# Emitting the assembly of the chunk inverses behind the products of the mixer's h and behind the first scores of retention

## The chip, the core and the metric

The kernel runs on one core of one Trainium2 chip. The metric is the device time of one execution in microseconds (us). A core has five engines, each with its own instruction stream, executed in order: TensorE (PE, with its weight loads shown as PEld), VectorE (DVE), ScalarE (ACT), GpSimd (POOL) and SyncE (SP), which here only issues DMAs. An instruction waits for semaphores of other engines or of DMAs, and everything behind it in the same stream waits with it.

## The reference

All values are float32; 512 tokens, width 1024. Two layers of a first kind of block (the second kind, which follows twice, isn't touched):

```python
for l in range(DEPTH):                       # DEPTH = 2
    ...                                      # a first feed-forward
    h = modulate(rms_norm(x), sh2, sc2)
    z = h @ w_in[l]
    z_a, z_b, z_c = split_cols(z, [RWKV_COLS, MLA_COLS, RET_COLS])
    o_a = rwkv7_mixer(z_a, ...)
    o_b = mla_mixer(z_b, ...)
    o_c = retention_mixer(z_c, ...)
    mixed = jnp.concatenate([o_a, o_b, o_c], axis=-1) @ w_out[l]
    x = x + g2[:, None, :] * mixed
    ...                                      # a second feed-forward
```

The rwkv mixer is a recurrence over tokens, with a state of 64x64 for each head and direction. Retention, per head and direction, is `scores = einsum(q, k) * dmat` and `einsum(scores, v)` over chunks; MLA is softmax attention over low-rank keys and values, with a rotary key `kpe` of 32 columns.

## The kernel before

A float32 product is written as three products of rounded halves (hi·hi, hi·lo, lo·hi). A weight lands by DMA in a buffer `raw`; ACT casts it to its high half, DVE or POOL subtracts that for the low half (both halves are tiles named `wr`), and PE multiplies. Weights come through a list, `self.wplan`, in a fixed order: `in_b` (five pieces), `in_kpe`, `w_uq_pe`, `w_ukv_v` (512 KB), `w_kq` (four pieces of 320 KB), then the output weights. Their DMAs are issued by SP, in stream with all other DMAs of SP.

The first mixer (`mixer1`, phase "mix1") runs two Python generators against each other in `merge`: the main one is `rwkv`, the other (`fill`) is everything else. Each `yield n` of the main one says how much other work is wanted at that place, and `merge` then draws on `fill`, whose own yields say how much they gave. The order in which calls are made, together with the allocator of tiles, sets the order of the engines' streams.

`fill` makes in turn: `rwkv_z` (the rwkv products with h), `ret_z` (the retention products), `mla_z` (the five `in_b` pieces and kpe, again products with h), `retention` (two head pairs j, with `mla_norms` between them), and `mla`. `retention` begins by making the stacks `kq` for its scores: casts on ACT and subtractions on DVE that write tiles named `mix_r_x`. Then, for each of four chunks c, it makes four score products on PE, two multiplications by the decay mask on DVE, and two value products one chunk later, and yields `RET_FILL` (2.5).

The main generator, `rwkv`, prepares the rwkv operands (`rwkv_prep`), calls `rwkv_inverse` and then runs the heads (`rwkv_heads`). `rwkv_inverse` inverts 64x64 triangular matrices, one for each chunk, head and direction: it takes 32x32 diagonal blocks through DRAM (`rw_d`) into another layout, inverts them on DVE by back substitution in `zb` (`mix_big_w`), and writes them back to DRAM. Two DMAs (`xa`) and sixteen DMAs of 32 KB (`xt`) on SP then bring the inverted blocks back. Behind these stands `yield INV_WAIT` (20), and then `rwkv_blocks` for j = 0 and 1, which assembles the off-diagonal blocks: for each j and direction 16 products of 32x32 (y), two copies on ACT, 16 products of 32x32 (z), two copies on ACT. That is 128 such products of 32x32 in all (the trace records each as two), and the heads begin after them. In the stream of PE before, the 20 units drawn at `INV_WAIT` end after `in_b[2]`; `in_b[3]`, `in_b[4]` and kpe, 24 matmuls each, are interleaved with the blocks and with the first work of the heads.

Of the kernel before, what the change touches and what calls it, by code (L numbers as in the profile page):

```python
# [37 lines left out]
RET_FILL = 2.5  # L38
# [197 lines left out]
class Build:  # L236
# [606 lines left out]
    def rwkv_inverse(self, os_):  # L843


        nc = self.nc
        dr, dz, dzt = (self.dram_p.tile([P, 1024], F32, tag=self.nm("rw_d"), name=self.nm("rw_d")) for _ in range(3))
        u = {}
        for j, o in enumerate(os_):
            for d in range(2):  # L850
                us = self.slot()
                u4 = us.rearrange("p (c h t) -> p c h t", c=4, h=2)
                pus = [self.aux_ps()[:, :256].rearrange("p (c t) -> p c t", c=4) for hh in range(2)]
                for par in range(2):
                    for c in range(4):
                        for hh in range(2):
                            rows = slice(hh * 64, hh * 64 + 64)
                            q = o["qm"][rows, d, c, par, par, :]
                            p = o["pr"][rows, d, c, 0, par * 64:par * 64 + 64]
                            a, b = (q, p) if d == 0 else (p, q)  # L860
                            nc.tensor.matmul(pus[hh][par * 64:par * 64 + 64, c, :], a, b, start=True, stop=True)
                for hh in range(2):
                    up = self.mask("tri")[:, :64].unsqueeze(1).to_broadcast([P, 4, 64])
                    nc.vector.scalar_tensor_tensor(u4[:, :, hh, :], pus[hh], -1.0, up, ALU.mult, ALU.mult)
                u[j, d] = us
                u3 = us.rearrange("p (m t) -> p m t", t=64)
                ud = self.slot()
                ud3 = ud[:, :256].rearrange("p (m t) -> p m t", t=32)
                for r0 in range(0, P, 32):
                    h0 = r0 % 64  # L870
                    nc.scalar.copy(ud3[r0:r0 + 32], u3[r0:r0 + 32, :, h0:h0 + 32])
                to = dr.rearrange("(j m d q) (r c) -> j d q r m c", j=2, m=8, d=2, r=32)[j, d]
                self.nc.sync.dma_start(to.rearrange("q r m c -> (q r) m c"), ud[:, :256].rearrange("p (m c) -> p m c", m=8))
                yield 2

        zb, zt = self.big_t(), self.big_t()
        self.nc.sync.dma_start(zb, dr)
        yield 6
        z3 = zb.rearrange("p (r c) -> p r c", r=32)
        for c in range(30, 0, -1):  # L880
            n = 31 - c
            tmp = self.small_t(256, "inv_t")
            t3 = tmp[:, :c * n].rearrange("p (r c) -> p r c", r=c)
            nc.vector.tensor_mul(t3, z3[:, 0:c, c:c + 1].to_broadcast([P, c, n]),
                                 z3[:, c:c + 1, c + 1:].to_broadcast([P, c, n]))
            nc.vector.tensor_add(z3[:, 0:c, c + 1:], z3[:, 0:c, c + 1:], t3)
            if c % 5 == 0:
                yield INV_STEP
        nc.vector.memset(zb[:, ::33], 1.0)
        self.nc.sync.dma_start(dz, zb)  # L890
        nc.vector.tensor_copy(zt.rearrange("p (c r) -> p c r", c=32), z3.rearrange("p r c -> p c r"))
        self.nc.sync.dma_start(dzt, zt)
        rows = lambda z, d: z.rearrange("(jm d q) (r c) -> d q r jm c", jm=16, d=2, r=32)[d]
        xa = []
        for d, z in enumerate((dzt, dz)):
            t = self.slot()
            self.nc.sync.dma_start(t.rearrange("p (m t) -> p m t", m=16), rows(z, d).rearrange("q r jm c -> (q r) jm c"))
            xa.append(t.rearrange("p (j m t) -> p j m t", j=2, m=8))
        xt = [[self.slot() for d in range(2)] for j in range(2)]
        for j in range(2):  # L900
            for d, z in enumerate((dz, dzt)):
                x3 = xt[j][d].rearrange("p (m t) -> p m t", t=64)
                for q in range(4):
                    r0, h0 = q * 32, q % 2 * 32
                    self.nc.sync.dma_start(x3[r0:r0 + 32, :, h0:h0 + 32], rows(z, d)[q, :, j * 8:j * 8 + 8, :])
                    if q % 2 != d:
                        nc.gpsimd.memset(x3[r0:r0 + 32, :, 32 - h0:64 - h0], 0.0)
        yield INV_WAIT
        for j in range(2):
            yield from self.rwkv_blocks(xt[j], [t[:, j] for t in xa], [u[j, d] for d in range(2)])  # L910
        return xt
# [450 lines left out]
    def retention(self, l, z, out, between):  # L1362
        nc = self.nc
        lg = self.small_t(16, "ret_lg")
        nc.scalar.activation(lg[:, 8:16], self.rows[:, 4 + 8 * l:12 + 8 * l], AF.Exp)
        nc.vector.tensor_scalar(lg[:, 0:8], lg[:, 8:16], -1.0, None, ALU.mult)
        lag = self.big_t()[:, :896]
        nc.sync.dma_start(lag, self.d["lag"])
        pn = self.aux_ps()
        kq = []  # L1370
        for j in range(2):
            dm = [self.ret_decay(lag, lg, j * 2 + hh) for hh in range(2)]
            py, pts = self.aux_ps(), None
            for c in range(5):
                if j == 0 and c in (0, 2):
                    kq.append((self.stack_q(z["k"][c // 2]), self.stack_k(z["q"][c // 2])))
                last = pts
                if c < 4:
                    scs, pts = [self.aux_ps() for hh in range(2)], []
                    for hh in range(2):  # L1380
                        self.stacked(scs[hh], *kq[j], hh, slice(c * P, (c + 1) * P), ALL)
                    for hh in range(2):
                        pt = self.slot()
                        nc.vector.scalar_tensor_tensor(pt, scs[hh], 0.125, dm[hh][:, 384 - c * P:896 - c * P],
                                                       ALU.mult, ALU.mult)
                        pts.append(pt)
                if c > 0:
                    for hh in range(2):
                        v = ((c - 1) % 2) * 256 + (j * 2 + hh) * 64
                        nc.tensor.matmul(py[hh * 64:hh * 64 + 64], z["v"][(c - 1) // 2][:, v:v + 64], last[hh],  # L1390
                                         start=c == 1, stop=c == 4)
                yield RET_FILL
            sq, o = self.slot(), z["g"][j]
            nc.scalar.activation(sq, py, AF.Square)
            nc.vector.scalar_tensor_tensor(o, py, self.v(f"gn_g{l}", j), o, ALU.mult, ALU.mult)
            yield 2.5
            self.head_sums(sq, pn, j * 8)
            yield 1
            if j == 0:
                yield from between  # L1400
        vv = self.small_t(64, "rs_v")
        nc.vector.tensor_scalar(vv[:, :16], pn[:, :16], 1.0 / 64, 1e-5, ALU.mult, ALU.add)
        rn = self.rsqrt(vv[:, :16], 16)
        yield 2
        for j in range(2):
            pb = self.head_bcast(rn[:, j * 8:j * 8 + 8], 2, 0)
            out[j] = z["g"][j]
            nc.vector.tensor_mul(out[j], out[j], pb)
            yield 1
# [16 lines left out]
    def mixer1(self, l):  # L1426
# [11 lines left out]
        def fill():  # L1438
            yield from self.rwkv_z(l, h, ps, dv, za)
            zc = yield from self.ret_z(l, h)  # L1440
            zb = yield from self.mla_z(l, h)
            yield from self.retention(l, zc, oc, self.mla_norms(l, zb))
            self.stage(2)
            yield from self.mla(l, zb, ob, (oa, oc))

        with self.phase("mix1"):
            self.stage(0)
            h, ps = self.modulated(1, [self.wget() for i in range(2)])
            self.lend_x()
            dv = self.derived(l)  # L1450
            self.merge(self.rwkv(l, za, dv, oa), fill())
            self.split_all((oa, oc))

            def update(j, po, sl):
                nc.vector.scalar_tensor_tensor(self.x[j][:, sl], po[:, sl], self.mod[:, 40 + j:41 + j],
                                               self.x[j][:, sl], ALU.mult, ALU.add)

            self.out_proj(lambda j: self.wget(), oa + oc + ob, update, "halves")
# [527 lines left out]
```

## Time and profile before

| | us |
|---|---|
| three runs | 3542.39, 3544.21, 3565.40 |
| their median | 3544.21 |
| the profiled execution, whole time | 3542.78 |
| its span | 3541.0 |
| PE busy in it | 3416.4 (96% of the span) |
| ACT busy, DVE busy | 1437.5, 2095.7 |
| mean granted TensorE clock | 0.982 |

The span is what the profiler sees between the first and last instruction; 1.8 us lie around it. Within the span, the first mixer's part of interest is at 526 to 606 us for layer 0 and at 1695 to 1767 us for layer 1. All operations are recorded by one helper, so every row has the same line (L138), and tiles are told by their names: `mix_h_x` is the h of the mixer, `mix_s`, `mix_s_x`, `mix_s_y` and `x` are scratch tiles, `mix_r_x` rounded operands, `mix_big_w` the wide tiles of the back substitution and of retention's decay masks, `ps` PSUM.

### The profile page before, as it was taken

How to read it: one execution, taken by the hardware profiler on the slowest of the kernel's cores; microseconds unless marked ns; L12 is line 12 of the kernel's file. 1: busy time of each engine (PE TensorE's matmuls, PEld its weight loads, DVE VectorE, ACT ScalarE, POOL GpSimd, SP SyncE). 2: the span in 40 equal slices, each digit the busy share in tenths (PEclk: the TensorE clock that was granted, in tenths of full speed). 3: DMA queues.
4: the chain of work that ended last, by engine and by line, in shares of the span. 5: the costliest groups of instructions: out<-in, count | busy, mean ns of one | idle time of the engine just before them, and what ended most of it. 6: DMA issues, size and time to landing. Idle time of an engine off the chain costs nothing. (4 is left out here: it accounts for less than half of the span.)

```text
span 3541.0 us, 45671 instructions
## 1 busy us (share of the span) xinstructions
PE 3416.4 (96%) x17394; PEld 2786.5 (79%) x17394; DVE 2095.7 (59%) x4153; ACT 1437.5 (41%) x2644; POOL 279.2 (8%) x344
## 2 busy tenths in 40 slices
PE   6999998999999999999899999999999999999998
PEld 5888876788888888887678888887788887778887
DVE  7954785757964544467576544466754446774445
ACT  3233554454233423245345423245443344444333
POOL 2000152100000000015310000000100000000000
PEclk9999998999999999999899999999999999999999
DMA  7933322015852222232201222221122222212222
GB/s 271 330 136 107 126 78 63 24 44 200 328 185 99 87 96 97 99 119 83 75 13 48 78 97 96 99 86 68 54 95 95 96 100 72 70 60 101 96 97 76
DMA packets 132876, 375.73 MB, mean 106 GB/s; under 512 B 37712, under 2 KB 41072, under 8 KB 132656
## 3 DMA queue, kind: packets, MB, share of 16 engines
q1 hardware_dynamic: 127808, 359.48, 29.5%
q0 software_dynamic: 3776, 12.32, 1.0%
q8 instruction: 136, 2.23, 0.2%
q10 hardware_dynamic: 1072, 1.01, 0.1%
q14 instruction: 84, 0.69, 0.1%
HBM read 362.27 MB, written 10.49 MB: 105 GB/s over the span
## 5 line engine op out<-in xcount | busy, mean ns | idle before, releaser
L138 ACT CAST wr<-raw 128x512 fp32r<-128x512 f32 (+2 forms) x1054 | 642.4, 611 | 1484.7 <-PE ps L138 1377.4
L138 DVE TENSOR_TENSOR wr<-raw,wr 128x512 fp32r<-128x512 f32 (+1 forms) x1004 | 681.0, 680 | 741.4 <-ACT wr L138 719.7
L138 PE MATMUL ps<-ff_h,wr 128*128 128x512 f32 (+1 forms) x4296 | 961.1, 385 | 9.9 <-ACT ff_h L138 7.4
L138 PEld LDWEIGHTS ps<-ff_h,wr 128*128 128x128 f32 x4296 | 794.8, 190 | 172.2 <-ACT ff_h L138 9.9
L138 PE MATMUL ps<-mlp_r,wr 128*128 128x512 f32 (+1 forms) x3120 | 699.3, 386 | 2.1 <-ACT mlp_r L138 2.1
L138 PEld LDWEIGHTS ps<-mlp_r,wr 128*128 128x128 f32 x3120 | 578.5, 188 | 121.2 <-ACT mlp_r L138 3.0
L138 PE MATMUL ps<-ff_r,wr 128*128 128x512 f32 (+1 forms) x2238 | 483.0, 377 | 0.0
L138 PEld LDWEIGHTS ps<-ff_r,wr 128*128 128x128 f32 x2238 | 403.6, 188 | 77.6
L138 PE MATMUL ps<-mix_r,wr 128*128 128x512 f32 (+1 forms) x1104 | 274.9, 399 | 2.4 <-DVE mix_s L138 1.8
L138 PE MATMUL ps<-mix_h_x,wr 128*128 128x512 f32 (+2 forms) x1104 | 261.1, 396 | 3.5 <-ACT mix_h_x L138 2.2
L138 PEld LDWEIGHTS ps<-mix_h_x,wr 128*128 128x128 f32 (+1 forms) x1104 | 202.5, 200 | 53.8 <-issue 4.5
L138 PEld LDWEIGHTS ps<-mix_r,wr 128*128 128x128 f32 (+1 forms) x1104 | 198.6, 185 | 56.1 <-issue 4.8
L138 DVE SCALAR_TENSOR_TENSOR ff_big<-ff_big,ff_big 128x1024 f32<-128x1024 f32 x144 | 176.6, 1238 | 15.2 <-DMA ff_big<-in_w_ada 14.5
L138 DVE SCALAR_TENSOR_TENSOR ff_s<-ff_s,ps 128x512 f32<-128x512 f32 x176 | 120.1, 683 | 82.2 <-PE ps L138 78.1
L138 DVE SCALAR_TENSOR_TENSOR x<-ps,hg,x 128x512 f32<-128x512 f32 (+1 forms) x102 | 73.3, 719 | 78.6 <-PE ps L138 78.4
L138 DVE TENSOR_TENSOR ps<-ps,mlp_s 128x512 f32<-128x512 f32 (+1 forms) x66 | 45.1, 683 | 100.4 <-PE ps L138 100.4
L138 ACT COPY mix_s<-ps 128x256 f32<-128x256 f32 (+7 forms) x156 | 61.6, 401 | 93.6 <-PE ps L138 60.4
L138 DVE TENSOR_TENSOR mlp_r<-mlp_s,mlp_r 128x512 fp32r<-128x512 f32 x80 | 54.6, 692 | 68.9 <-ACT mlp_r L138 68.9
L138 ACT ACTIVATE mix_s<-ps,m 128x512 f32<-128x512 f32 (+3 forms) x140 | 70.8, 528 | 50.7 <-PE ps L138 25.9
L138 PE MATMUL ps<-mix_s,mix_s 128*128 128x128 f32 (+7 forms) x648 | 86.4, 288 | 2.1 <-ACT mix_s L138 1.4
L138 POOL MEMSET mix_s<- 32x256 f32 (+3 forms) x36 | 12.6, 349 | 956.9 <-DVE mix_r L138 353.8
L138 PEld LDWEIGHTS ps<-mix_s,mix_s 128*128 128x128 f32 (+5 forms) x648 | 65.4, 172 | 18.6 <-ACT mix_s L138 8.0
(317 smaller groups left out, 3451.0 us busy)
## 6 DMA issues: line engine op xcount, KB each, us to landing
raw<-in_ff_in SPq DMA_DIRECT2D x176, 512.0 KB, 3.4
ff_big<-in_w_ada SPq DMA_DIRECT2D x144, 512.0 KB, 6.3
raw<-in_mlp SPq DMA_DIRECT2D x128, 512.0 KB, 3.4
raw<-in_ff_out SPq DMA_DIRECT2D x64, 448.0 KB, 3.2
raw<-in_ff_out SPq DMA_DIRECT2D x32, 512.0 KB, 3.6
raw<-in_out SPq DMA_DIRECT2D x32, 512.0 KB, 3.4
raw<-in_in SPq DMA_DIRECT2D x28, 512.0 KB, 3.4
raw<-in_in_a SPq DMA_DIRECT2D x18, 512.0 KB, 4.0
```

The source lines that it names most:

```text
L138: self.alloc.last[self.name] = f(*a, **k)
```

## The change

Three insertions. `mixer1` clears a flag, `retention` sets it when it begins, and `rwkv_inverse`, behind `INV_WAIT`, yields until the flag is set and then once more `RET_FILL`:

```diff
@@ rwkv_inverse
         yield INV_WAIT
+
+        while not self.ret_begun:
+            yield 1
+        yield RET_FILL
         for j in range(2):
             yield from self.rwkv_blocks(xt[j], [t[:, j] for t in xa], [u[j, d] for d in range(2)])
@@ retention
         pn = self.aux_ps()
         kq = []
+        self.ret_begun = True
         for j in range(2):
@@ mixer1
             self.stage(0)
+            self.ret_begun = False
             h, ps = self.modulated(1, [self.wget() for i in range(2)])
```

No computation is added or removed. SP's stream is the same; those of the other engines hold the same work in another order, in both layers alike.

On PE, before, these rows stand where `in_b[2]` ends (products with the weights wr_73 and wr_74) and `in_b[3]` begins (wr_77 and wr_78); the 32x32 rows are the first y of the blocks and then its z:

```order
L138 MATMUL ps_116<-mix_1_h_x_15_2744,wr_74 128x512
L138 MATMUL ps_116<-mix_1_h_x_14_2743,wr_73 128x512
L138 MATMUL ps_118<-mix_1_s_y_4_2724,mix_1_s_2680 32x32 x16
L138 MATMUL ps_113<-mix_1_h_x_0_2729,wr_77 128x512
L138 MATMUL ps_113<-mix_1_h_x_1_2730,wr_77 128x512
L138 MATMUL ps_113<-mix_1_h_x_0_2729,wr_78 128x512
L138 MATMUL ps_113<-mix_1_h_x_2_2731,wr_77 128x512
L138 MATMUL ps_113<-mix_1_h_x_3_2732,wr_77 128x512
L138 MATMUL ps_112<-mix_1_s_2686,mix_1_s_y_1_2721 32x32 x8
```

In the changed kernel the products of `in_b[3]`, `in_b[4]` and kpe follow `in_b[2]` directly, 72 rows without a break. Then PE has these rows: the last of kpe (32x512), the eight score matmuls of chunks 0 and 1 (two `mix_1_r_x` operands), two value products, and the first 32x32:

```order
L138 MATMUL ps_113<-mix_1_h_x_15_2744,wr_80 32x512
L138 MATMUL ps_113<-mix_1_h_x_14_2743,wr_79 32x512
L138 MATMUL ps_115<-mix_1_r_x_2_4013,mix_1_r_x_0_4011 128x512
L138 MATMUL ps_116<-mix_1_r_x_2_4013,mix_1_r_x_0_4011 128x512
L138 MATMUL ps_115<-mix_1_r_x_4_4015,mix_1_r_x_0_4011 128x512
L138 MATMUL ps_117<-mix_1_r_x_3_4014,mix_1_r_x_1_4012 128x512
L138 MATMUL ps_116<-mix_1_r_x_4_4015,mix_1_r_x_0_4011 128x512
L138 MATMUL ps_117<-mix_1_r_x_4_4015,mix_1_r_x_1_4012 128x512
L138 MATMUL ps_118<-mix_1_r_x_3_4014,mix_1_r_x_1_4012 128x512
L138 MATMUL ps_118<-mix_1_r_x_4_4015,mix_1_r_x_1_4012 128x512
L138 MATMUL ps_114<-mix_1_s_x_2_4003,mix_1_s_2675 64x512
L138 MATMUL ps_112<-mix_1_s_y_4_2724,mix_1_s_2680 32x32 x16
```

(Between the last two rows shown there is one more value product, which reads alike.) The 32x32 of the blocks moved behind 72 products with h, eight scores and two value products; between the later groups of 32x32 there now stand scores and value products of the following chunks.

On ACT, before, these rows stand at the same place. `raw_65` holds `w_ukv_v` here and `raw_63` the first piece of `w_kq`; the two casts of `mix_1_r_x` at the end are the first of the stacks that the scores read, and the copies are those of the blocks (32x256, 32x8x32) and of the products with h:

```order
L138 COPY x_127<-ps_117 128x512
L138 CAST wr_71<-raw_65 128x512
L138 COPY mix_1_s_2665<-ps_116 32x8x32 x2
L138 COPY mix_1_s_2669<-ps_118 32x256 x2
L138 CAST wr_76<-raw_65 128x512
L138 COPY mix_1_s_2664<-ps_112 32x8x32 x2
L138 CAST wr_70<-raw_63 128x512
L138 COPY mix_1_s_y_2_2722<-ps_114 128x4x64
L138 COPY mix_1_s_y_3_2723<-ps_114 64x2x128 x2
L138 CAST wr_80<-raw_63 128x128
L138 CAST mix_1_r_x_0_4188<-mix_1_s_2667 64x512
L138 CAST mix_1_r_x_1_4189<-mix_1_s_2667 64x512
```

(Two copies 128x4x64 are between the last copy shown and the cast of wr_80.) In the changed kernel:

```order
L138 COPY x_129<-ps_118 128x512
L138 COPY x_127<-ps_112 128x512
L138 CAST wr_71<-raw_65 128x512
L138 CAST wr_76<-raw_65 128x512
L138 CAST wr_70<-raw_63 128x512
L138 CAST wr_80<-raw_63 128x128
L138 CAST mix_1_r_x_0_4011<-mix_1_s_2667 64x512
L138 CAST mix_1_r_x_1_4012<-mix_1_s_2667 64x512
L138 CAST mix_1_r_x_2_4013<-mix_1_s_2679 64x512 x2
L138 CAST mix_1_r_x_3_4014<-mix_1_s_2679 64x512 x2
```

The copies of the blocks have gone from between the casts. The order among the casts is the same in both kernels: two of `w_ukv_v`, two of `w_kq[0]`, then the stacks of the scores.

On DVE, in the changed kernel, these rows make the low halves of the same weights (from raw_65 and raw_63), the rotary turn of kpe (from ps_113, two rows), and the low halves of the first stacks:

```order
L138 TENSOR_TENSOR wr_72<-raw_65,wr_71 128x512
L138 TENSOR_TENSOR wr_75<-raw_65,wr_76 128x512
L138 TENSOR_TENSOR wr_69<-raw_63,wr_70 128x512
L138 TENSOR_TENSOR wr_79<-raw_63,wr_80 128x128
L138 STREAM_SHUFFLE mix_1_s_x_0_4001<-ps_113 32x512
L138 TENSOR_TENSOR mix_1_s_x_1_4002<-ps_113,mix_1_s_2674 32x512
L138 TENSOR_TENSOR mix_1_r_x_0_4011<-mix_1_s_2667,mix_1_r_x_0_4011 64x512
```

Before, the same weights' low halves stood there too, with work of the blocks and of the heads between them.

## Rows read from the trace of the kernel before

**Rows 1.** Waits of PE over the span: waiter, releaser; us, times, longest.
```profile
PE ps L138 <- DMA mix_s_y<-rw_d: 24.5, 2, 12.3
```

**Rows 2.** Timeline of PE, layer 0: start, us, engine, operation, tiles, [idle before].
```profile
526.62 16.51 PE L138 MATMUL ps<-mix_h_x,wr 128*128 128x512 f32 x72
555.46 1.70 PE L138 MATMUL ps<-mix_s_y,mix_s 32*32 32x32 f32 x32 [12.33 <-DMA mix_s_y<-rw_d]
...
563.07 6.32 PE L138 MATMUL ps<-mix_h_x,wr 128*128 128x512 f32 x16
...
585.15 5.84 PE L138 MATMUL ps<-mix_h_x,wr 128*32 128x512 f32 x24
...
595.25 0.68 PE L138 MATMUL ps<-mix_s_x,mix_s_x 64*64 64x64 f32 x16 [0.88 <-DVE mix_s_x L138]
...
605.60 1.79 PE L138 MATMUL ps<-mix_r_x,mix_r_x 128*128 128x512 f32 x4
...
736.20 0.60 PE L138 MATMUL ps<-ident,mix_s 128*128 128x128 f32 x4
...
782.23 0.48 PE L138 MATMUL ps<-mix_r_x,wr 128*128 128x512 f32 x1
```

**Rows 3.** Timeline of PE, layer 1.
```profile
1695.41 16.51 PE L138 MATMUL ps<-mix_h_x,wr 128*128 128x512 f32 x72
1724.06 1.69 PE L138 MATMUL ps<-mix_s_y,mix_s 32*32 32x32 f32 x32 [12.14 <-DMA mix_s_y<-rw_d]
...
1731.67 5.75 PE L138 MATMUL ps<-mix_h_x,wr 128*128 128x512 f32 x16
...
1761.81 0.68 PE L138 MATMUL ps<-mix_s_x,mix_s_x 64*64 64x64 f32 x16 [0.87 <-DVE mix_s_x L138]
```

**Rows 4.** Stretches: sum; PE, PEld, DVE, ACT, POOL (x); granted clock; DMA; GB/s.
```profile
547.00:548.00 1.00, 0.00 (x0) 0.00 (x0) 0.99 (x1) 0.00 (x0) 0.97 (x2) 0.89 0.33 135
568.00:569.00 1.00, 1.00 (x5) 0.82 (x4) 0.00 (x0) 0.00 (x0) 0.00 (x0) 0.87 0.00 0
581.00:582.00 1.00, 1.00 (x34) 0.88 (x31) 0.16 (x1) 0.78 (x2) 0.00 (x0) 0.95 0.00 0
585.00:586.00 1.00, 1.00 (x7) 0.60 (x6) 0.22 (x1) 0.95 (x4) 0.00 (x0) 0.84 0.03 10
1735.00:1736.00 1.00, 1.00 (x5) 0.79 (x4) 0.00 (x0) 0.00 (x0) 0.00 (x0) 0.70 0.66 261
```

**Rows 5.** Timeline of SP's DMA issues, both layers.
```profile
561.32 0.40 SPq L138 DMA_DIRECT2D raw<-in_w_ukv_v  x1
561.82 27.19 SPq L138 DMA_DIRECT2D raw<-in_w_kq  x4
...
1731.12 0.40 SPq L138 DMA_DIRECT2D raw<-in_w_ukv_v  x1
```

**Rows 6.** DMA issues, 540 to 600 us: KB each, median us to landing.
```profile
raw<-in_w_kq SPq DMA_DIRECT2D x4, 320.0 KB, 3.6
raw<-in_w_ukv_v SPq DMA_DIRECT2D x1, 512.0 KB, 3.8
```

**Rows 7.** Timeline of POOL, layer 0, the low half of a weight.
```profile
551.30 1.73 POOL L138 TENSOR_TENSOR wr<-raw,wr 128x512 fp32r<-128x512 f32 x1 [1.84 <-ACT wr L138]
```

**Rows 8.** Timeline of DVE, layer 0.
```profile
591.04 0.72 DVE L138 STREAM_SHUFFLE mix_s_x<-ps 32x512 f32<-32x512 f32 x1
591.66 0.66 DVE L138 TENSOR_TENSOR mix_s_x<-ps,mix_s 32x512 f32<-32x512 f32 x1
...
595.14 2.12 DVE L138 TENSOR_TENSOR mix_r_x<-mix_s,mix_r_x 64x512 fp32r<-64x512 f32 x3
```

**Rows 9.** ACT by line and form, 500 to 600 us: busy us, mean ns.
```profile
L138 ACT CAST wr<-raw 128x512 fp32r<-128x512 f32 x19 | 11.5, 617 | 14.5 <-PE ps L138 14.1
L138 ACT CAST mix_r_x<-mix_s 64x512 fp32r<-64x512 f32 x7 | 4.3, 617 | 1.4 <-PE ps L138 1.3
L138 ACT CAST wr<-raw 128x128 fp32r<-128x128 f32 x1 | 0.3, 298 | 1.7 <-PE ps L138 1.7
```

## The prediction

> **What bounds the kernel now.** PE is busy for 96% of the span, so first the waits of PE were read. One of the largest is a DMA: [rows 1] twice some 12 us, 24.5 in all, for `mix_s_y` from `rw_d`. The timeline of PE shows where: in layer 0 the 72 products of `in_b[0..2]` run from 526.62 to 543.13, 0.229 us each, and then nothing runs for 12.33 us until the first 32x32 of the blocks [rows 2]; in layer 1 the same, 12.14 us from 1711.92 on [rows 3]. PE's stream is in order, and 72 more products with h stand behind the waiting row.
>
> Next the granted clock was read. [...] At the lower level half of the time is lost, so the present loss is
>
> layer 0: 12.33 + (568.26 - 555.46)/2 + (585.32 - 581.90)/2 + 0.88 (a wait of the first heads for DVE [rows 2]) = 12.33 + 6.40 + 1.71 + 0.88 = 21.3 us;
> layer 1: 12.14 + (1735.60 - 1724.06)/2 + 0.87 [rows 3] = 18.8 us.
>
> Together 40.1 us, 1.1% of the span. No change of this place can bring more.
>
> **The change part by part.** Nothing is added or removed; SP's stream is the same, and so are its DMAs' issue times as long as nothing before them moves. What moves on PE: the 72 products of `in_b[3]`, `in_b[4]` and kpe come directly behind `in_b[2]`, then eight scores and two value products of retention, and only then the first 32x32. The old wait thus goes: the blocks' DMAs have landed by 555.46 [rows 2], and PE does not come to them before 570 (below). The question is whether PE has its operands for what now stands there. Step by step, layer 0:
>
> `in_b[3]`: 24 x 0.229 = 5.5, to 548.6. `in_b[4]` takes the same, but its 15th product needs a low half that POOL ends at 551.30 + 1.73 = 553.03 [rows 7] (it is behind the cast of ACT, behind that engine's work on retention's masks, which does not move). 10 products are then left: 555.3. kpe: 5.84 [rows 2], to 561.2. Without that wait it would be 560.0; **1.2 us are lost**.
>
> The scores need the stacks `mix_r_x`. The stacks' data have long been there, but on ACT their casts stand behind those of `w_ukv_v` and of `w_kq[0]`. Before, that cost nothing, since PE came to the first score only near 594. SP issues `w_ukv_v` at 561.32, when it is done with the 16 `xt` transfers, and it takes 3.8 us to land [rows 5, 6]: 565.1. The first `w_kq` is issued at 561.82, 3.6 us to landing, 565.4, which is earlier than its turn. ACT then: three casts of 512 columns at 0.617 and one at 0.298 [rows 9], to 567.25; two stacks and the two halves of a third, 4 x 0.617 [rows 9], to 569.7. DVE makes the low halves behind each cast: with 0.71 for each (the stacks' rows, 2.12 for three [rows 8]) it is done with the weights at 565.7 + 3 x 0.71 + 0.3 = 568.1, then shuffles and multiplies kpe, 0.72 + 0.66 [rows 8], to 569.5, then the low half of the first stack, 0.71: 570.2. Both engines thus end near 570.1, and the first score starts there: **a new wait of 570.1 - 561.2 = 8.9 us**. It is the old wait in a smaller form, with a weight's landing in the place of the blocks'. In layer 1 `w_ukv_v` is issued at 1731.12 [rows 5], 19.2 us after `in_b[2]` ends, where it is 18.2 in layer 0: 9.9 us.
>
> Bounds of that wait: none if the stacks came ahead of the weights, which the streams exclude; 8.5 to 11 with a landing of 3.6 or one of 5 to 6 (the `xt` transfers end shortly before).
>
> After a wait of that length I expect the lower level again, as the old one had it 4.7 us after the last product [rows 4]. The scores and values take 1.79 / 4 = 0.45 us each [rows 2], so the ten of them at half speed are 9 us of unbroken work, longer than the 5.2 after which the return came before. **Cost: 5.2 / 2 = 2.6 us** (bounds: 1.9 by layer 1's 3.9 us; above, a rival below).
>
> [...]
>
> The blocks themselves: 128 products of 32x32 as before, and between their stages ACT's copies; before, PE shows no idle time among them, and now scores and values stand between. 0, by these rows. The first heads' wait for DVE stays: 0.9. The heads begin some 20 us of filler later, but what the filler has done ahead is missing behind: from the last head's transposes (736.20) to the output product (782.23) there are 46 us of MLA [rows 2], which cover that. 0 here; without that cover up to 10 us.
>
> Sum: layer 0 loses 1.2 + 8.9 + 2.6 + 0.9 = 13.6 instead of 21.3, layer 1 14.6 instead of 18.8: 7.7 + 4.2 = 11.9 us gained. From the profiled execution's 3542.8 (span 3541.0 and 1.8 around it) that is 3530.9; the median of the runs is 1.4 above that execution, so 3532, or with a little for waits not seen, **3533 us**.
>
> **The rivals.** Slower: *the clock stays low through scores and blocks.* For it: before, from 555.46 to 563.07 PE had no idle time and products with h lay between the 32x32, and the clock did not return; it did in both layers only in a run of 16 products without 32x32 [rows 2, 3], and it fell again at 581.90 among small products [rows 4]. Against it: ten unbroken large ones come first. If it fails, 16 scores and 8 values (24 x 0.45 = 10.8 at full speed) and the blocks (eight times 1.70 / 2 = 0.85 [rows 2], 6.8) run at half speed, 17.6 us lost instead of 2.6: 15 more in a layer. In one layer: 3548; in both: 3563. It decides the sign from 6 us more per layer on.
>
> Full gain: *the stall goes and nothing takes its place*, ACT being ahead because its copies for the blocks have left. Then about 2 us are lost per layer: 40.1 - 4 = 36 us gained, 3507. Against it stands the landing at 565.1.
>
> *Given back elsewhere:* the heads' tail is exposed, 5 us in each layer, or the scores' wait is nearer 14 than 9: no net change, 3543.
>
> **How the numbers follow.** Forecast (a shorter wait, low level for about 5 us): 0.55, 3533, own range 3524 to 3540. Slower rival: 0.20 for one layer or half of it in both (3541 to 3550), 0.08 for both (to 3563). Full gain: 0.08, 3507. Given back: 0.09. The range leaves out the full gain and half of the last of the slower cases: 3514 to 3556. About 1% (35 us) is what a measurement of this kernel can tell from no change: faster by over that needs nearly the whole 40.1 us: 0.06; slower by over that needs more than both layers at the lower level: 0.02; the rest, 0.92, lies within.
>
> **What would show it.** In the profile after: `in_b[3]`, `in_b[4]` and kpe directly behind `in_b[2]` at 0.23 us each; no wait for `rw_d`; a wait of PE of 8 to 11 us ahead of the first score, released by DVE or ACT `mix_r_x`, its casts behind those of `wr` from `w_ukv_v`; a granted clock of 0.5 for 4 to 5 us after it. It would be wrong if that wait is absent (full gain) or if the 0.5 lasts through the last 32x32 (slower rival).

## The result and the profile after

The changed kernel takes 3572.76 us (median of 13 runs, 3561.95 to 3582.82), beside 3542.39 for the kernel before (13 runs in the same rounds): ratio 1.0081, 95% interval 1.0067 to 1.0095. It is slower by 0.8%, some 29 us by that ratio, where 3533 had been forecast. The profiled execution has a span of 3565.1 us, 24.1 more than before. The first mixer of layer 1 begins 12.7 us later than before (its first products with h stand at 1708.08 in the rows below, at 1695.41 in [rows 3]), of which 12.2 came up in layer 0's mixer and the layer's rest; the other 11.4 come later.

Waits of PE after the change (waiter, releaser; us, times, longest):

```profile
PE ps L138 <- DVE mix_r_x L138: 19.8, 4, 8.8
...
PE ps L138 <- POOL wr L138: 1.6, 2, 0.8
```

The wait for `rw_d` of [rows 1] is gone. In its place stands one for the stacks of the scores. PE's timeline shows where, in layer 0 and at the start of layer 1's mixer:

```profile
533.95 27.14 PE L138 MATMUL ps<-mix_h_x,wr 128*128 128x512 f32 x118 [0.82 <-POOL wr L138]
569.89 1.19 PE L138 MATMUL ps<-mix_r_x,mix_r_x 128*128 128x512 f32 x2 [8.80 <-DVE mix_r_x L138]
572.20 3.68 PE L138 MATMUL ps<-mix_r_x,mix_r_x 64*128 64x512 f32 x6 [1.12 <-DVE mix_r_x L138]
...
577.72 1.73 PE L138 MATMUL ps<-mix_s_y,mix_s 32*32 32x32 f32 x32
...
591.31 0.79 PE L138 MATMUL ps<-mix_r_x,mix_r_x 64*128 64x512 f32 x1
...
615.22 1.01 PE L138 MATMUL ps<-mix_s_y,mix_s_x 64*64 64x64 f32 x16
616.16 0.50 PE L138 MATMUL ps<-mix_r,mix_r_x 128*128 128x512 f32 x1
...
1708.08 6.08 PE L138 MATMUL ps<-mix_h_x,wr 128*128 128x512 f32 x26
```

All 144 products with h stand together and end at 561.09 (533.95 + 27.14). Then nothing runs for 8.80 us, and the first score starts at 569.89. ACT's timeline says why: it sits without work until `w_ukv_v` has landed, and casts it and `w_kq` ahead of the stacks.

```profile
564.48 1.86 ACT L138 CAST wr<-raw 128x512 fp32r<-128x512 f32 x4 [8.02 <-DMA raw<-in_w_ukv_v]
566.24 4.46 ACT L138 CAST mix_r_x<-mix_s 64x512 fp32r<-64x512 f32 x7
...
568.47 4.40 DVE L138 TENSOR_TENSOR mix_r_x<-mix_s,mix_r_x 64x512 fp32r<-64x512 f32 x4
```

(The last row is from DVE's timeline: the low halves of the stacks.) So far this is the forecast nearly to the tenth. What was not forecast is in the granted clock (stretches of 1 us; the last three columns are granted clock, DMA share and GB/s):

```profile
564.00:565.00 1.00, 0.00 (x0) 0.00 (x0) 0.00 (x0) 0.52 (x1) 0.00 (x0) 0.92 1.03 389
...
616.00:617.00 1.00, 1.00 (x13) 0.89 (x9) 0.00 (x0) 0.38 (x1) 0.00 (x0) 0.98 0.00 0
766.00:767.00 1.00, 0.30 (x1) 0.31 (x2) 1.00 (x3) 0.62 (x1) 0.00 (x0) 0.61 0.00 0
783.00:784.00 1.00, 1.00 (x6) 0.88 (x5) 0.14 (x2) 0.58 (x1) 0.00 (x0) 0.85 0.00 0
```

It falls to 0.5 at 564.8 in the wait, and every stretch from there to 616.0 shows 0.50: through the scores, the blocks and the first heads, 45.0 us of work (46.1 less the wait of 1.12). Before, it was 12.8 us [rows 4]. It comes back among products of 64x64, not behind a run of large ones. In layer 1 it is the same, from 1745.8 to 1797.0. A second stretch at 0.5 lies in attention, from 766.2 to 783.3.

### The profile page after: what moved, and what is told of

Read it like the earlier page. It is cut to its first block, busy times and chain, and to the rows that moved or that the text cites. A ratio compares the mean times of both kernels' runs of the same rounds, so it can differ in the third digit from the quotient of the medians.

```text
span 3565.1 us, 45666 instructions
## 1 busy us (share of the span) xinstructions
PE 3450.8 (97%) x17394; PEld 2811.2 (79%) x17394; DVE 2094.8 (59%) x4153; ACT 1438.4 (40%) x2644; POOL 279.2 (8%) x344
## 4 chain that ended last, share of the span: by engine, by line
PE 85%; DVE 10%; ACT 2%; issue 1%; POOL 1%; DMA 1%; SPq 1%; ACTq 0%; DVEq 0%; POOLq 0%
PE ps L138 85%; DVE mix_s L138 2%; DVE m L138 1%; DVE mix_big_w L138 1%; DVE wr L138 1%; DVE x L138 1%; ACT mix_s L138 1%; DVE mix_rw L138 1%; DVE mix_r_x L138 1%; DVE mix_s_y L138 1%; SPq L138 1%; ACT mix_r L138 0%; DVE ff_big L138 0%; ACT wr L138 0%; DVE sq L138 0%
## 5 line engine op out<-in xcount | busy, mean ns | idle before, releaser
L138 PE MATMUL ps<-mix_h_x,wr 128*128 128x512 f32 (+2 forms) x1104 | 252.9, 390 | 4.7 <-ACT mix_h_x L138 2.2
L138 PE MATMUL ps<-mix_s,mix_s 32*32 32x32 f32 (+7 forms) x776 | 96.3, 281 | 3.8 <-ACT mix_s L138 2.4
L138 PEld LDWEIGHTS ps<-mix_s,mix_s 128*128 128x128 f32 (+6 forms) x776 | 74.7, 173 | 23.8 <-ACT mix_s L138 8.4
```

The source lines that it names most:

```text
L138: self.alloc.last[self.name] = f(*a, **k)
```

## Experiments

Two things lie in the changed order: a wait of 8.8 us, and a long stretch of small products without the products with h that stood between them. Scores, values, the 32x32 and the heads' first products are called small here and the products with h large; where the line between the two lies is not shown (see *Open*). The experiments take away one, the other, or both. Their kernels are named by their labels. "Before" is the kernel before, run beside each; the last column gives where layer 0's clock was at the lower level between 545 and 630 us (stretches of over 5 us), from the profiled execution. That is one execution of each; only the changed kernel was profiled twice. The medians are of 5 to 13 runs, in e5 of two.

| kernel | median us | ratio to before (95%) | wait before blocks or scores | lower level |
|---|---|---|---|---|
| before | 3539 to 3542 | 1 | 12.33 | 547.8 to 568.3 |
| changed | 3572.76 | 1.0081 (1.0067 to 1.0095) | 8.80 | 564.8 to 616.0 |
| e1_stacks_first | 3543.57 | 0.9997 (0.9980 to 1.0014) | 2.79 | 561.6 to 599.2 |
| e2_blocks_first | 3534.46 | 0.9980 (0.9970 to 0.9991) | 0.45, 1.87 | 563.2 to 597.4, 611 to 617.9 |
| e3_fill_wait | 3550.64 | 1.0021 (1.0011 to 1.0030) | none | 586.3 to 610.2 |
| e4_all_scores | 3556.33 | 1.0063 (1.0037 to 1.0088) | 8.13 | 567.9 to 626 |
| e5_dense_between | 3573.29 | 1.0090 (1.0070 to 1.0110) | 0.53, 1.83 | 574.4 to 581.2 |
| e6_no_blocks | 3526.16 | 0.9960 (0.9947 to 0.9973) | none | none |
| w28 | 3561.74 | 1.0043 (1.0019 to 1.0067) | none | 559.4 to 569.7, 573.1 to 593.6 |
| w26 | 3555.35 | 1.0038 (1.0024 to 1.0052) | 6.02 | 550.6 to 560.8, 577.9 to 588.1, 605.2 to 618.8 |
| e7_one_dense | 3523.76 | 0.9950 (0.9934 to 0.9966) | 0.47 | 605.3 to 612.1 |
| e8_two_dense | 3541.23 | 0.9985 (0.9968 to 1.0003) | none | 611 to 628 |
| e9_after_dense | 3554.67 | 1.0034 (1.0015 to 1.0052) | 9.16 | 563.5 to 590.8 |

**The wait taken away: e1_stacks_first.**

```diff
+                    if c == 0:
+                        self.stacks = [self.alloc.last[e].ins for e in ("scalar", "vector")]
...
-        wv = self.wget()
+        with self.tc.issue_after(self.stacks[0]), self.tc.issue_after(self.stacks[1]):
+            wv = self.wget()
```

(The first call for `w_kq` is wrapped alike. PE's stream stays that of the changed kernel but for scores that change places with neighbouring groups of 32x32.)

> The changed kernel with one difference: on ACT and DVE the casts and subtractions of w_ukv_v and w_kq are put behind the first stacks of retention's scores, so that the scores don't wait for the landing of w_ukv_v. Theory A (the 8.8 us wait ahead of the scores drops TensorE to its lower level, and the small products behind it don't bring it back until 616 us): the first score moves from 569.9 to about 564, the wait is 2.5 to 3.5 us, the granted clock stays 1.0 through scores and blocks, and about 6 us of wait and 22.5 us of lower level go in each layer: some 57 us below the changed kernel, 3508, about 34 below the kernel before. Theory B (the new order of scores, values and 32x32 does not keep the clock up by itself): the wait shrinks by 6 us in each layer, but the clock falls to 0.5 among the blocks all the same: about 3550.

```profile
562.44 1.19 PE L138 MATMUL ps<-mix_r_x,mix_r_x 128*128 128x512 f32 x2 [2.79 <-DVE mix_r_x L138]
```

```profile
561.00:562.00 1.00, 0.00 (x0) 0.00 (x0) 0.99 (x1) 0.98 (x2) 0.92 (x2) 0.81 0.75 251
599.00:600.00 1.00, 1.00 (x11) 1.00 (x9) 0.00 (x0) 0.96 (x5) 0.00 (x0) 0.92 0.00 0
```

(One row of PE's timeline, and stretches with the granted clock.) The wait is 2.79 us as expected, and the time falls by 29 us against the changed kernel; but the clock falls all the same, at 561.6, inside that shorter wait, and stays down for 37.6 us until 599.2. Theory A falls here: the long lower level does not need the long wait. That it needs no wait at all this run does not show. The measured 3544 is nearer to B's 3550 than to A's 3508. Its runs lie in two groups, from 3530 to 3533 and from 3542 to 3550, and the profiled one is of the first.

**The wait filled with work: e3_fill_wait.**

```diff
         self.ret_begun = True
+        pd = self.aux_ps()
+        with self.tc.issue_after(self.alloc.last["tensor"].ins):
+            for i in range(16):
+                nc.tensor.matmul(pd, self.ident, self.masks[:, :512], start=True, stop=True)
```

> The changed kernel with 16 products of identity and masks (float32, 512 columns, about 8 us) added on TensorE between kpe and the first score; their result is not read. They fill the wait of 8.8 us with work and move nothing else. Theory A (the wait drops the clock): the first score starts at 570 as in the changed kernel, at the full level, and the 22.5 us that the lower level costs in each layer go, although work was added: about 45 us below the changed kernel, 3520. Theory B (the order of the small products drops it): no gain, 3565.

```profile
559.42 13.90 PE L138 MATMUL ps<-masks,ident 128*128 128x512 f32 x32
572.76 3.79 PE L138 MATMUL ps<-mix_r_x,mix_r_x 128*128 128x512 f32 x8
...
585.59 0.50 PE L138 MATMUL ps<-mix_r_x,mix_r_x 64*128 64x512 f32 x1
```

```profile
586.00:587.00 1.00, 1.00 (x5) 0.20 (x4) 0.69 (x1) 0.95 (x3) 0.58 (x2) 0.64 0.00 0
610.00:611.00 1.00, 1.00 (x20) 0.89 (x16) 0.00 (x0) 0.75 (x2) 0.00 (x0) 0.91 0.06 16
```

The 16 products took 13.9 us instead of 8, so the scores start 3 us late. PE is not idle once from 532.4 to past 610, and still the clock falls, at 586.3, in value products between the fourth and the fifth group of 32x32, and comes back at 610.2, among products of 64x64 as in the changed kernel. Neither theory had this: the wait brings the fall forward (564.8 instead of 586.3), and the order by itself brings one too. Even so 22 us are gained against the changed kernel, with 28 us of added work.

This run also prices the lower level. From the first score to the score row at 591.31 the changed kernel takes 21.4 us, 20.3 without its wait of 1.12; here the same rows take 12.8 (572.76 to 585.59), all at 1.0. The lower level thus takes 7.5 of 20.3, 37%, and not half: the rows differ (a group of 32x32 is 1.73 us in the changed kernel and 1.09 in e3 and e7; four value rows are 1.98 us there and 1.08 in e3, which is nearly double). By that price, an estimate for the heads' rows, the 45.0 us of the changed kernel cost 16.6, by half of the time 22.5.

**The blocks left out: e6_no_blocks** (e3 with the 32x32 replaced by zeros; part of the inverse is missing).

```diff
-            py = self.aux_ps()
...
             for par in range(2):
                 f, s2 = slice(par * 64, par * 64 + 32), slice(par * 64 + 32, par * 64 + 64)
...
+                nc.gpsimd.memset(x3[f, :, 32:64] if d == 0 else x3[s2, :, 0:32], 0.0)
```

> As e3, but the 32x32 products of the blocks are left out: their places are set to zero, so that part of the inverse is missing. Theory C1 (the 32x32 drop the clock): without them it stays at 1.0 through scores, values and the first heads; against e3 8 us of work and 12 us of lower level go in each layer, about 3512. Theory C2 (values, transposes and the first heads are small enough alone): the clock still falls some 5 to 10 us after the last score, and 8 to 12 us go in each layer, about 3535.

No stretch between 475 and 741 us shows less than 1.0: scores, values, transposes and the first heads run at the full level, one behind the other. C1 is right about the clock: without the 32x32 there is no fall, in layer 1 either, but for 3.4 us from 1712 among products with h. Whether it is the form of the 32x32 or the 8.7 us by which the stretch is shorter, the run does not separate. The time is 24 us below e3's (31 between the profiled executions), where 40 were expected: by the price found in e3 the 24 us at the lower level cost 9 in a layer and not 12, and 8 us of work are gone, 34 in all; the other 10 are not explained. The fall in attention is there in both (743 to 760 here, 760 to 777 in e3).

**Longer runs of scores: e4_all_scores.** One number: `yield RET_FILL * 4` in place of `yield RET_FILL`.

> The changed kernel with the blocks of 32x32 behind all four chunks of retention's first head pair, so that behind the wait 16 scores and 8 values stand unbroken. The wait of 8.8 us stays. Theory A1 (the 32x32 between the scores keep the clock low): it returns some 5 us into the scores, at about 575, and some 20 us in each layer go: about 3525. Theory A2 (scores and values that wait for one another don't bring it back either): it stays at 0.5 through scores, blocks and the first heads as in the changed kernel: 3560 to 3570.

```profile
572.04 1.62 PE L138 MATMUL ps<-mix_r_x,mix_r_x 128*128 128x512 f32 x3 [8.13 <-DVE mix_r_x L138]
574.34 3.68 PE L138 MATMUL ps<-mix_r_x,mix_r_x 64*128 64x512 f32 x6 [0.69 <-DVE mix_r_x L138]
577.96 1.97 PE L138 MATMUL ps<-mix_s_x,mix_s 128*64 128x512 f32 x4
...
590.44 1.73 PE L138 MATMUL ps<-mix_s_y,mix_s 32*32 32x32 f32 x32
...
1756.05 3.69 PE L138 MATMUL ps<-mix_r_x,mix_r_x 64*128 64x512 f32 x6 [0.69 <-DVE mix_r_x L138]
...
1772.15 1.35 PE L138 MATMUL ps<-mix_s_y,mix_s 32*32 32x32 f32 x32
```

In layer 0, from 574.34 to 590.44 PE does scores and values without idle time and without a 32x32, 16.1 us, and the clock stays at 0.5, until 626. This is A2, and it is the step that the prediction had counted on: scores and values did not bring the clock back here within 16 us, where it had counted on 5. In layer 1 they stand without idle time from 1756.05 to 1772.15, again at 0.5, but there the clock was back at 1772.8, 0.65 us into the first group of 32x32, and fell again at 1776.3. So it is not shown that they could not bring it back at all. The median, 3556, is 4 us below A2's range.

**Large products between the blocks: e9_after_dense, e5_dense_between.** The changed kernel with one unread product of identity and masks ahead of each group of 32x32 (e9):

```diff
+    def dense(self):
+        pd = self.aux_ps()
+        for i in range(1):
+            self.nc.tensor.matmul(pd, self.ident, self.masks[:, :512], start=True, stop=True)
...
             with self.tc.issue_after(self.alloc.last["tensor"].ins):
+                self.dense()
                 for par in range(2):
...
+            with self.tc.issue_after(self.alloc.last["tensor"].ins):
+                self.dense()
             pz = self.aux_ps()
```

> The changed kernel with one unread product of identity and masks in front of each of the eight groups of 32x32, and nothing else; the wait of 8.8 us ahead of the scores stays. Theory C (the wait lowers the clock, and the stretch of small products behind it holds it low until 616): with these products in between, the clock returns within some 12 us of the first score, about 582, instead of 46; 7 us of added work replace some 12 us of loss in a layer, about 3562 where the changed kernel has 3572. Rival (one such product per group is enough to hold the clock up, as in e7, but not to bring it back): 0.5 until 616 and beyond, and 14 us more work at half speed in each layer: 3600.

```profile
569.47 1.19 PE L138 MATMUL ps<-mix_r_x,mix_r_x 128*128 128x512 f32 x2 [9.16 <-DVE mix_r_x L138]
...
577.30 2.08 PE L138 MATMUL ps<-masks,ident 128*128 128x512 f32 x2
...
589.42 1.81 PE L138 MATMUL ps<-masks,ident 128*128 128x512 f32 x2
591.15 1.09 PE L138 MATMUL ps<-mix_s,mix_s_y 32*32 32x32 f32 x32
```

```profile
590.00:591.00 1.00, 1.00 (x2) 0.00 (x0) 0.00 (x0) 0.00 (x0) 0.00 (x0) 0.59 0.00 0
```

The wait stays, 9.16 us, and so does the fall in it. But the clock is back at 590.8, in the third of the added products, 21 us after the first score instead of 46, and stays up through the other blocks (from 591.15 on a group takes 1.09 again). In layer 1 it is the same: back at 1768.4, 22 us after the first score, at the end of the third added product. 18 us are gained on the changed kernel, with eight products added in each layer. Theory C had the return at 582, so later than expected, with a time better than expected.

e5 has ten such products ahead of the scores and two ahead of each group.

> As e3, but ten unread products of identity and masks ahead of the scores and two more in front of each of the eight groups of 32x32 (26 in all, 0.87 us each at the full level; e3 had 16). Theory C (what drops the clock in e3 at 586 and holds it low in the other kernels is the stretch of small products without large ones between them): the granted clock stays at 1.0 through all blocks, the 12.4 us of loss by the lower level that e3 has in a layer go, and 10 more products cost 8.7 us of which 5.2 were delay ahead of the scores: about 3546, with no 0.5 before the heads. Theory D (the clock falls a certain time after the h products, whatever comes): it falls at about 586 as in e3, and the time is 3552 plus some 17 to 25, about 3573.

```profile
574.00:575.00 1.00, 1.00 (x3) 0.47 (x2) 0.90 (x3) 0.00 (x0) 0.00 (x0) 0.71 0.00 0
581.00:582.00 1.00, 1.00 (x18) 0.48 (x19) 0.00 (x0) 0.00 (x0) 0.00 (x0) 0.88 0.00 0
```

The clock fell at 574.4, behind two waits of 0.53 and 1.83 us, came back at 581.2 in the first pair of added products, and stayed at 1.0 through all eight groups, as C says; the 6.8 us at 0.5 ahead of them C did not have. The time, from two runs, is what D expected, 3573: against e3 there are ten more products in each layer, and a stretch at 0.5 from 697 to 725 us, among the heads, that e3 doesn't have. By its time alone this run tells nothing.

**A version that is faster than both: e2_blocks_first, e7_one_dense, e8_two_dense.** e2 puts the blocks directly behind kpe, ahead of the scores:

```diff
-INV_WAIT = 20
+INV_WAIT = 36
```

(in the kernel before, with e1's order of the casts).

> The kernel before with INV_WAIT 36 instead of 20 and with the weights' casts behind the stacks as in e1: the blocks stand directly behind kpe, ahead of the scores. Theory A: the blocks' inputs land at about 562.6 where kpe ends at 561.1, a wait of 1.5 to 2 us, ACT's copies follow at once, no wait is over 3 us, the clock stays at 1.0: about 3508 as e1. Theory B (small 32x32 products near the h products lower the clock by themselves, as at 581.9 in the kernel before): the lower level comes back within the blocks, 3520 to 3545.

No wait is over 1.87 us, and yet the clock falls at 563.2, in that wait, and comes back only at 597.4: B, and not A, with a time inside B's range. e2 is 6 us faster than before. With one added product per group (e7), and two (e8):

> e2 (blocks directly behind kpe, ahead of the scores) with one unread product of identity and masks (0.87 us at the full level) in front of each of the eight groups of 32x32. Theory C (small products without large ones between them bring the lower level; e2 had 0.5 from 564 to 598, some 16 us of loss in a layer): if one per group is enough, the clock stays at 1.0 through the blocks, 7 us of work replace 16 us of loss: about 3515, faster than both kernels although work is added. If one is too few: the same 0.5 as in e2 and 14 to 20 us more, 3550.

> As e7 with two such products per group, as many as in e5, where the clock stayed at 1.0 from 582 through all blocks. Theory C: 1.0 through the blocks; 14 us of work replace 16 us of loss in a layer: about 3530, the same as e2. Theory D (the clock falls whatever stands there): 3558.

```profile
561.18 1.09 PE L138 MATMUL ps<-mix_s_y,mix_s 32*32 32x32 f32 x32
562.20 1.12 PE L138 MATMUL ps<-masks,ident 128*128 128x512 f32 x2
...
585.75 1.09 PE L138 MATMUL ps<-mix_s_y,mix_s 32*32 32x32 f32 x32
...
1721.43 2.08 PE L138 MATMUL ps<-masks,ident 128*128 128x512 f32 x2
1723.43 1.73 PE L138 MATMUL ps<-mix_s,mix_s_y 32*32 32x32 f32 x32
...
1742.27 1.09 PE L138 MATMUL ps<-mix_s,mix_s_x 32*32 32x32 f32 x32
```

(PE's timeline of e7.) In layer 0, from the first group to the last each takes 1.09 us: full level through all blocks. In layer 1 the clock fell all the same, at 1721.4, behind the second group and the scores that follow it, and the third to the fifth stand at 0.5 (1.73 us each) with an added product ahead of each; it came back at 1741.9, in the sixth added product. So one product per group held the level in one layer of two. The kernel takes 3523.76 in all, 0.5% below the kernel before and 11 us below e2, though eight products are added in each layer. Two per group hold the clock through the blocks of both layers (at 1.0 until 611.0 in layer 0 and until 1774.9 in layer 1) but cost as much as they give: 3541 beside 3539 for before. Later stretches at 0.5 remain in both kernels, in e7 from 605.3 to 612.1 and from 1769.2 to 1786.3.

**Fewer h products moved: w26, w28** (the kernel before with `INV_WAIT` 26 or 28).

> The kernel before with INV_WAIT 26: only in_b[3] stands ahead of the blocks, in_b[4] and kpe lie between them as before. The wait shrinks from 12.3 to about 6.9 us. Theory C: the clock falls in it as before, returns some 5 us into in_b[4]'s 24 products, and falls again near the last blocks, as at 581.9 before; about 7 us less in each layer: 3525 to 3532. Theory A: the same up to the last blocks, no later fall: 3522.

> The kernel before with INV_WAIT 28 instead of 20: in_b[3] and in_b[4] stand ahead of the blocks, kpe's 24 products between their first groups; no wait for the scores, which come later. The wait of 12.3 us is filled up to 555.3, where the blocks' inputs land: it is 0 to 1 us. Theory A (only long waits drop the clock): 1.0 throughout, about 36 us below the kernel before, 3505. Theory C: full level until kpe's products end, then the last blocks and first heads with no large products behind them fall to 0.5 for 20 to 35 us in each layer: 21 of loss are replaced by 10 to 18, 3520 to 3537.

```profile
554.52 1.70 PE L138 MATMUL ps<-mix_s_y,mix_s 32*32 32x32 f32 x32 [6.02 <-DMA mix_s_y<-rw_d]
556.14 7.93 PE L138 MATMUL ps<-mix_h_x,wr 128*128 128x512 f32 x24
```

(PE's timeline of w26.) In w26 the wait halves, to 6.02 us, and the clock returns in the 24 products of `in_b[4]`, at 561; then it falls again at 577.9 and at 605, and the kernel is 0.4% slower than before, where every theory had expected faster. In w28 there is no wait at the blocks; the clock falls at 559.4, among the first 32x32, returns at 569.7, at the end of 17 kpe products in one run, and falls again at 573.1 behind them. In layer 1 a wait of 3.43 us stands among its blocks instead, and the clock falls in that, at 1754.1. Its runs spread from 3531 to 3572, the median is 3562, where A had expected 3505 and C 3520 to 3537. In neither did the shorter wait bring a gain; where exactly the clock then falls was not foreseen by C either.

**The changed kernel once more: after_again.**

> The changed kernel as it is, profiled once more. If the second stretch at 0.5 in the tail of attention (766 to 783 us, and 1181 us later in layer 1), for which the rows show no other cause than waits of 0.95 and 1.27 us that e1 has too without a fall, belongs to the kernel, it is there again at the same place in both layers; if it is a matter of the single execution, it is not.

The span is 3565.1 again. The stretch behind the wait is there again in both layers (563.3 to 614.5, and 1751.1 to 1802.3), so it belongs to the kernel. The later ones are of the execution: none at 766 now, but 696.4 to 723.7 and 778.3 to 792, and in layer 1 only a short one at 1819.

## Why the prediction was wrong

*The old wait* was read rightly: with the products moved ahead, PE does not wait for `rw_d` any more, in either layer.

*The new wait.* Forecast 8.9 us ahead of a first score at 570.1; measured 8.80 at 569.89, by the chain that was worked out: landing of `w_ukv_v`, four casts, the stacks, DVE's low halves. That it came out to the tenth is in part luck: ACT began at 564.48 instead of 565.1 and DVE came to the first stack at 568.47 instead of 569.5, but a low half took 1.10 us there (4.40 for four) instead of 0.71. In layer 1 9.9 were forecast and 8.82 measured: `w_ukv_v` landed no later there in relation to the products. POOL's 1.2 became 0.82 at an earlier weight, and the 1.12 before the third score was missing from the sum. The first heads' 0.9 did not come: between 593 and 616 PE has no idle time. Together, 10.7 us measured stand against 11.0 forecast in layer 0.

*The step that failed* is the cost of the lower level behind that wait: "Cost: 5.2 / 2 = 2.6 us", from the statement that ten scores and values at half speed are "longer than the 5.2 after which the return came before". The 5.2 is read from the trace of before, where the clock stood at 0.50 from 547.8, 4.7 us after the last product (543.13 [rows 2]), and came back at 568.26, by the 0.87 of the stretch 568 to 569 [rows 4], 5.2 us into the run of 16 products with h from 563.07 [rows 2]; in layer 1 it was 3.9 us, from 1731.67 to 1735.60 [rows 3, rows 4]:

```profile
548.00:549.00 1.00, 0.00 (x0) 0.00 (x0) 0.33 (x1) 0.00 (x0) 1.00 (x1) 0.50 1.02 422
...
567.00:568.00 1.00, 1.00 (x4) 0.73 (x3) 0.00 (x0) 0.00 (x0) 0.00 (x0) 0.50 0.00 0
```

The time of a run was taken over from a run of other products. The 16 products with h of before had the clock back in 5.2 us; 16 us of scores and values in e4 did not in layer 0, and in layer 1 it was back only behind them. The term measured 16.6 us (priced by e3) to 22.5 (half of the time) in each layer instead of 2.6. No run shows a lower level that ends 5.2 us into scores and values. The half of the time was that of the 16 products with h, which took 6.32 us [rows 2] where 16 x 0.229 = 3.66 are due, 2.66 too much in those 5.2; the mixed rows lost 37% of theirs (7.5 of 20.3 us, e3).

*The slower rival* named this mechanism and its mark (0.5 through the last 32x32), and had 0.08 for both layers at 3563; the profiled execution took 3567, the median is 3573. Its price of 15 was near, by two errors that offset. Its end was set at the last block, where the stretch ran on through the first heads. And it took half of a group of 32x32 for lost, where the trace of before has such a group at both levels, 1.70 us at 555.46 [rows 2] and 1.09 behind the return:

```profile
569.33 1.09 PE L138 MATMUL ps<-mix_s,mix_s_y 32*32 32x32 f32 x32
```

Its weight was too low: the trace of before held two signs, a fall at 581.90 among small products and a first return only in a run of products with h [rows 4, rows 2], and "ten unbroken large ones come first" was an argument, not a row.

*What was not seen at all* is that the 72 products with h were more than filler. They stood between the 32x32 and, with kpe's 24, between them and the first heads; moved to the front, they leave some 40 us of small products in one piece. e3 shows the fall without any wait, e6 that it goes with the 32x32, e9 that large products put back between them end it earlier (in both layers), e8 and, in layer 0 alone, e7 that they keep it away. Not every fall has a wait ahead of it: that at 564.8 lies in the wait of 8.80 us, that at 586.3 in e3 came where PE was never idle.

*The sum for layer 0.* Before 21.3 us were lost here, with the clock at 0.50 from 547.8 to 568.3 and from 581.9 to 585.3 [rows 4]. After: 0.8 + 8.8 + 1.1 in waits and 16.6 to 22.5 at the lower level, 27 to 33, and 6 to 8 for the stretch from 766.2 to 783.3. That is 12 to 20 more, where 12.2 were measured. With the lower level of before priced by e3 too (19.2 instead of 21.3), it is 14 to 20, so the sum is a little too large. The other stretches at 0.5 up to the next mixer add up to 34 us in both kernels and cancel.

*Open.* What in a product counts for the clock is not shown. Half of the scores' rows are 128*128 by 512 like the products with h and the added ones; the 17 kpe products in whose run w28's clock came back are 128*32, narrower than the values (128*64). Nor is it large products alone that bring it back: in the changed kernel and in e3 it returned among products of 64x64 of the heads (at 616.0 and 610.2), and the second return of before, at 585.32, is 0.17 us into the run of kpe [rows 2]. Why one added product per group held the level in layer 0 of e7 and not in layer 1 is open. The stretch in attention: e1 has rows and waits of the same form there (0.95 and 1.27 us) and no fall, and the changed kernel had it in one execution and not in the other. Why w26 and w28 are slower than before is told by their stretches, not explained.

## What to carry to other kernels

Before large products are moved away from small ones, ask what they do for the clock there (e9: with one ahead of each group it returned at 590.8 instead of 616.0), and not only what they hide. A wait that is removed in one place counts only with the level at which the work behind it runs (here 12.33 us of wait became 8.80, and 12.8 us of work at 0.5 became 45.0), and that is priced from a row of the same products, at both levels, not from half of the time. If a stretch of small products has to stand alone, a few unread large products in it can pay for themselves (e7: 0.5% faster, though its clock still fell in one layer), but only a few (e8: the level held in both layers, and nothing gained).

## What the runs showed of the hardware

- The granted clock fell from 1.0 to 0.5 on a TensorE that had not been idle for 53 us (e3, at 586.3), in value products between groups of 32x32, and with the 32x32 left out it did not there (e6, 1.0 from 475 to 741).
- Scores and values for 16.1 us without idle time did not raise it (e4, layer 0; in layer 1 it rose 0.65 us behind them). With one product of 128x128 by 512 added ahead of each group it rose in the third of them, in both layers, 21 and 22 us after the first score instead of 46 (e9).
- The same single product per group kept it from falling among the blocks in layer 0 and not in layer 1 (e7, at 1721.4); two kept it there in both (e8, at 1.0 until 611.0 and 1774.9).
- The lower level cost 37% of the time of a mixed stretch (20.3 us against 12.8 for the same rows), not 50%: groups of 32x32 take 1.73 us against 1.09.
- Two executions of the same kernel with the same span had their later stretches at 0.5 in different places (766 to 783, or 696 to 724 and 778 to 792).
